# One stationary tile for both token halves: pair scores of a gated recurrence with the second half laid out in reverse

## The chip, the cores and the metric

The kernel runs on one core of a Trainium2 chip. The metric is the device time of one execution in microseconds (us), the median of several runs. The core has five engines with a queue each: TensorE (matmuls; PE in the profile, its weight loads PEld), VectorE (DVE), ScalarE (ACT), GpSimd (POOL), and SyncE (SP), which here issues the DMAs.

## What is computed

One layer of a streaming encoder on 1024 tokens of width 1024, all in float32: half a SwiGLU feed-forward block, a mixer with two groups of heads side by side, cross attention to 256 memory tokens, and another half block. The change is in the mixer. Its first group is a gated linear recurrence (4 heads of width 128), its second stick-breaking attention (8 heads of width 64). Cut to what matters:

```python
# recurrent heads: f is a gate per token and channel, k = 1 - f
#   S_t = diag(f_t) S_{t-1} + outer(k_t, i_t),    o_t = S_t^T q_t
# within a chunk this is
a = jnp.einsum('bhtd,bhsd,bhtsd->bhts', qt, kt, decay)      # decay = product of the gates between s and t, s <= t
o_intra = jnp.einsum('bhts,bhsv->bhtv', a, vt)
o_inter = jnp.einsum('bhtd,bhdv->bhtv', qt * jnp.exp(bt), state)
new_state = jnp.exp(b_last)[..., None] * state + jnp.einsum('bhsd,bhsv->bhdv', k_dec, vt)

# stick-breaking heads, strictly causal, z = q.k / sqrt(d)
#   A[t,s] = sigmoid(z_ts) * prod_{s<j<t} (1 - sigmoid(z_tj)),    o = A v
```

## The kernel before, in words

Activations lie transposed: channels on the 128 partitions, tokens along the free dimension, in two halves of H = 512 tokens, so every tensor comes as a half 0 and a half 1 (`hf`). Projections are sums of three matmuls (`mm3`, lines 125 to 129) of operands split into a high and a low part; a matmul on plain float32 operands appears in the profile as two instructions.

The mixer runs over four pairs p of stick-breaking heads and four recurrent heads n, woven by `interleave` (lines 142 to 150): it runs one generator step by step and between its steps a due share of a second generator's units. For each p there are two stages (lines 1443 to 1457). In the attention stage `sb_attend(p)` is woven with the projection `hg_proj(p)` of recurrent head p (48 units). In the recurrent stage `hg_attend(p)` (30 steps) is woven with `sb_proj(p + 1)` (64 units of three or six matmuls); for the last head with `memory()`, the projection of the memory tokens (128 units). The order on each engine's queue is settled when the kernel is built, from source order and dependencies.

**`hg_attend`** (lines 1281 to 1377) treats chunks of 128 tokens (index j, four to a half). Scores between a query and a key need the product of the gates between them, and the kernel builds these by doubling. `scores` (line 1289) gives the plain products, of which the diagonal is kept (line 1319) in a tile A per half, keys on partitions, queries along the free dimension. Then, for m = 1, 2, 4, ..., 64, neighbouring blocks of m tokens form pairs: a key of the first block of a pair meets a query of the second. `pair_scores(hf, m)` computes these scores. For m up to 16 (line 1309) it multiplies all 128 keys of a chunk, as the stationary operand, with the 64 queries that lie in second blocks (picked with strides), and VectorE copies the valid blocks into A with a predicated copy and a mask (line 1313). For m of 32 and 64 (line 1302) it multiplies only the m keys of one block with the m queries of its partner, block by block, and ScalarE copies each result to A (line 1304). After each level VectorE multiplies the queries of the second blocks by the product of the gates of their partner (line 1330), the keys of the first blocks likewise (line 1331), and the products of the gates pairwise (line 1333). All this is done for half 0 and then for half 1 at each level, one step of the weave each. At the end the keys are transposed (line 1340), and the state is carried from chunk to chunk in order of time (lines 1345 to 1363).

Each level's matmuls use as stationary operand keys of one half, of which at m up to 16 only every other block is a key block; the masks drop the rest.

**`sb_attend`** (lines 1103 to 1239): for each block t of 128 queries `z_steps` computes the scores with all earlier keys, two sigmoids, masks the diagonal block on GpSimd (line 1129), forms the running product from the latest key to the earliest with a scan over a reversed view (line 1132) and multiplies (line 1134). A query block of half 1 does this first for the keys of half 1, then for those of half 0, with the product carried over. `turn` transposes the weights, `values` multiplies them with v.

The masks of `pair_scores` are made at the start on GpSimd (lines 513 to 522): 5 fills and 10 selects of 128x64.

Of the kernel before, what the change touches and what calls it, by code (L numbers as in the profile page):

```python
# [18 lines left out]
P = 128  # L19
T = 1024  # L20
# [11 lines left out]
def hybrid_layer(ctx, tc, x, x_cols, mem, gains, ffn1_w_gu, ffn1_w_down, w_in, w_out, mem_w_q, mem_w_kv, mem_w_o,  # L32
# [397 lines left out]
    with ExitStack() as st:  # L430
# [83 lines left out]
        for m in (1, 2, 4, 8, 16):  # L514
            mk = maskp.tile([P, P // 2], F32, name=f"mask{m}")
            nc.gpsimd.memset(mk, 1.0)
            nb = P // (2 * m)
            nc.gpsimd.affine_select(out=mk, in_=mk, compare_op=ALU.is_ge, fill=0.0, base=0,
                                    pattern=[[-2 * m, nb], [0, m]], channel_multiplier=1)
            nc.gpsimd.affine_select(out=mk, in_=mk, compare_op=ALU.is_ge, fill=0.0, base=m - 1,  # L520
                                    pattern=[[2 * m, nb], [0, m]], channel_multiplier=-1)
            masks[m] = mk
# [518 lines left out]

    def sb_proj(p, r):
# [24 lines left out]
        for jj in range(4):  # L1067
            ps = psa.tile([P, 2, 2 * P], F32, name="acc")
            for q in range(2):
                t0 = (2 * jj + q) % 4 * P  # L1070
                hh = hT[jj // 2]
                for k in range(DC):
                    wh, wl = units[k // 4]
                    lhs = (hh[k][0][:, t0:t0 + P], hh[k][1][:, t0:t0 + P])
                    mm3(ps[:, q, :], lhs, (wh[:, k % 4, :], wl[:, k % 4, :]), k == 0, k == DC - 1)
                    if k % 2:
                        yield
            v = sbk.tile([P, 2, 2 * P], F32R, name=("v0h", "v0l", "v1h", "v1l")[jj])
            iv = hgp.tile([P, 2, P], F32, name=f"i{jj}")
            for q in range(2):  # L1080
                y = ys[jj // 2][:, (2 * jj + q) % 4:(2 * jj + q) % 4 + 1]
# [21 lines left out]
    def sb_attend(p, r, rest):  # L1103
# [5 lines left out]
        def z_steps(hf, e, g):  # L1109
            for t in (2 * g, 2 * g + 1):  # L1110
                width = (t + 1) * P
                carry = None
                qs = slice(t % 4 * P, t % 4 * P + P)
                q = r["q", t // 4][e]
                for s0 in ((0,) if width <= H else (H, 0)):
                    n = min(width - s0, H)
                    nn = max(n, 2 * P)
                    k, kl = r["k", s0 // H][e], r["kl", s0 // H][e]
                    z = psz.tile([P, H], F32, name="z")
                    nc.tensor.matmul(z[:, 0:nn], q[:, qs], k[:, 0:nn], start=True, stop=False)  # L1120
                    nc.tensor.matmul(z[:, 0:nn], q[:, qs], kl[:, 0:nn], start=False, stop=True)
                    om = sbp.tile([P, H], F32, name="om", bufs=2)
                    b = b_tile(p)
                    nc.scalar.activation(om[:, 0:n], z[:, 0:n], AF.Sigmoid, scale=-0.125)  # L1124
                    nc.scalar.activation(b[:, 0:n], z[:, 0:n], AF.Sigmoid, scale=0.125)
                    if carry is None:
                        dg = slice(n - P, n)
                        for a, fill in ((om, 1.0), (b, 0.0)):
                            nc.gpsimd.affine_select(out=a[:, dg], in_=a[:, dg], compare_op=ALU.is_gt, fill=fill,  # L1129
                                                    base=0, pattern=[[-1, P]], channel_multiplier=1)  # L1130
                    rev = om[:, n - 1::-1]
                    nc.vector.tensor_tensor_scan(rev, rev, rev, 1.0 if carry is None else carry,  # L1132
                                                 op0=ALU.mult, op1=ALU.bypass)
                    nc.vector.tensor_tensor(b[:, 0:n - 1], b[:, 0:n - 1], om[:, 1:n], op=ALU.mult)
                    if carry is not None:
                        nc.vector.tensor_tensor(b[:, n - 1:n], b[:, n - 1:n], carry, op=ALU.mult)
                    carry = om[:, 0:1]
# [3 lines left out]
        def turn(hf, e, g, jj):  # L1141
# [3 lines left out]
            offs = {2 * jj: 2 * P if diag else 0, 2 * jj + 1: 0 if diag else 2 * P}  # L1145
            for j in (2 * jj, 2 * jj + 1):
                for t in (2 * g, 2 * g + 1):
                    if j > t:
                        continue
                    c0 = offs[j] + (t % 2) * P  # L1150
                    nc.tensor.transpose(tr[:, c0:c0 + P], w[hf, e, t, j // 4][:, j % 4 * P:j % 4 * P + P], ident)
            lo = P if diag else 0
            wh = sbk.tile([P, H], F32R, name="wh", bufs=2)
            wl = sbk.tile([P, H], F32R, name="wl", bufs=2)
            if diag:
                nc.gpsimd.memset(wh[:, 0:P].bitcast(F32), 0.0)
                nc.gpsimd.memset(wl[:, 0:P].bitcast(F32), 0.0)
            nc.scalar.activation(wh[:, lo:H], tr[:, lo:H], AF.Copy)
            nc.vector.tensor_tensor(wl[:, lo:H], tr[:, lo:H], wh[:, lo:H].bitcast(F32), op=ALU.subtract)
            return wh, wl, offs  # L1160

        def values(hf, e, g, jj, turned, first):
            wh, wl, offs = turned
            for j in (2 * jj, 2 * jj + 1):
                ws = slice(offs[j], offs[j] + 2 * P)
                vv = r["v", jj][:, j % 2, e * P:(e + 1) * P]
                oo = halfway[hf, e][:, g % 2 * 2 * P:(g % 2 + 1) * 2 * P]
# [84 lines left out]
    def hg_proj(n, r):  # L1252
        uq, uf, ug = [load_cols(mw, w_in, [c0 + P * n]) for c0 in (0, 512, 1536)]
        for hf in range(2):
            ps = psa.tile([P, H], F32, name="acc")
            yield from proj_steps(ps, uq, hT[hf])
            r["hq", hf] = hgp.tile([P, H], F32, name="hq", bufs=2)
            nc.vector.tensor_tensor(r["hq", hf], ps, rs[hf], op=ALU.mult)
        for hf in range(2):
            ps = psa.tile([P, H], F32, name="acc")  # L1260
            yield from proj_steps(ps, uf, hT[hf])
            f = hgp.tile([P, H], F32, name="hf", bufs=2)
            k = hgp.tile([P, H], F32, name="hk", bufs=2)
# [4 lines left out]
            r["hf", hf], r["hk", hf] = f, k  # L1268
        for hf in range(2):
# [3 lines left out]
            sg = hgp.tile([P, H], F32, name="hA", bufs=2)  # L1273
# [7 lines left out]
    def hg_attend(n, r):  # L1281
        sl = [slice(j * P, (j + 1) * P) for j in range(4)]
        A, tots = {}, {}

        def scores(hf):
            a = psz.tile([P, H], F32, name="z")
            k, q = r["hk", hf], r["hq", hf]
            for j in range(4):
                nc.tensor.matmul(a[:, sl[j]], k[:, sl[j]], q[:, sl[j]], start=True, stop=True)
            return a.rearrange("p (j t) -> p j t", j=4)  # L1290

        def pair_scores(hf, m):
# [3 lines left out]
            k = r["hk", hf]  # L1296
            if m >= 32:
                for b in range(nb):
                    rows = slice(2 * m * b, 2 * m * b + m)
                    for j in range(4):  # L1300
                        k0 = j * P + 2 * m * b
                        nc.tensor.matmul(a[rows, j * m:(j + 1) * m], k[:, k0:k0 + m], r["hq", hf][:, k0 + m:k0 + 2 * m],
                                         start=True, stop=True)
                    nc.scalar.activation(A[hf][rows, :, 2 * m * b + m:2 * m * (b + 1)],
                                         a[rows, 0:4 * m].rearrange("p (j t) -> p j t", j=4), AF.Copy)
                return
            q = r["hq", hf].rearrange("p (j b h r) -> p j b h r", j=4, h=2, r=m)[:, :, :, 1, :]
            for j in range(4):
                nc.tensor.matmul(a[:, j * 64:(j + 1) * 64], k[:, sl[j]], q[:, j], start=True, stop=True)  # L1309
            dst = A[hf].rearrange("p j (b h r) -> p j b h r", h=2, r=m)[:, :, :, 1, :]  # L1310
            src = a[:, 0:4 * 64].rearrange("p (j b r) -> p j b r", j=4, r=m)
            mk = masks[m].bitcast(U32).unsqueeze(1).broadcast_to([P, 4, 64]).rearrange("p j (b r) -> p j b r", r=m)
            nc.vector.copy_predicated(dst, mk, src)

        for hf in range(2):
            A[hf] = hgp.tile([P, 4, P], F32, name="hA", bufs=2)
            a = scores(hf)
            q, f = r["hq", hf], r["hf", hf]
            nc.vector.tensor_tensor(A[hf], a, ident.unsqueeze(1).broadcast_to([P, 4, P]), op=ALU.mult)
            nc.vector.tensor_tensor(q, q, f, op=ALU.mult)  # L1320
            tots[hf] = f
            yield
        for m in (1, 2, 4, 8, 16, 32, 64):
            for hf in range(2):
                nb = H // (2 * m)
                tv = tots[hf].rearrange("p (b h) -> p b h", h=2)
                qv = r["hq", hf].rearrange("p (b h r) -> p b h r", h=2, r=m)[:, :, 1, :]
                kv = r["hk", hf].rearrange("p (b h r) -> p b h r", h=2, r=m)[:, :, 0, :]
                pair_scores(hf, m)
                nc.vector.tensor_tensor(qv, qv, tv[:, :, 0:1].broadcast_to([P, nb, m]), op=ALU.mult)  # L1330
                nc.vector.tensor_tensor(kv, kv, tv[:, :, 1:2].broadcast_to([P, nb, m]), op=ALU.mult)
                nt = r["hf", hf][:, 0:nb]
                nc.vector.tensor_tensor(nt, tv[:, :, 0], tv[:, :, 1], op=ALU.mult)
                tots[hf] = nt
                yield
        for hf in range(2):
            k = r["hk", hf]
# [7 lines left out]
        for hf in range(2):  # L1345
            o = pso.tile([P, H], F32, name="so")
            ds = psz.tile([P, H], F32, name="z")
            k, q = r["hk", hf], r["hq", hf]
            for j in range(4):
                iv = r["i", 2 * hf + j // 2][:, j % 2, :]  # L1350
                nc.tensor.matmul(ds[:, sl[j]], k[:, sl[j]], iv, start=True, stop=True)
                nc.tensor.matmul(o[:, sl[j]], iv, A[hf][:, j, :], start=True, stop=state is None)
# [5 lines left out]
                else:  # L1358
                    nc.vector.scalar_tensor_tensor(ns, state, tots[hf][:, j:j + 1], ds[:, sl[j]], op0=ALU.mult, op1=ALU.add)
# [347 lines left out]
```

## Time and profile before

| | |
|---|---|
| median of 3 runs | 2291.49 us (2290.48 to 2295.58) |
| the profiled execution | 2291.69 us; span from first to last instruction 2290.0 us, mean granted TensorE clock 0.992 |
| TensorE matmul busy | 2216.7 us, 97% of the span |
| VectorE, ScalarE, GpSimd busy | 73%, 43%, 32% |
| recurrent heads 0 to 3 | about 791 to 856, 934 to 995, 1073 to 1134, 1212 to 1290 us |
| attention pairs 1 to 3 | about 856 to 934, 995 to 1073, 1134 to 1212 us |

How to read it: a row of a group or a timeline names engine, source line, operation, output tile <- input tiles, shapes, and a count (x8: eight instructions in a row). In a timeline the first number is the start in us from the span's start, the second the time until the last of the group ends; for TensorE ends are modelled, so distances between starts are what counts. "[0.93 <-PE z L1309]" is idle time of the engine ahead of the instruction and what ended it. L82 and L127 to L129 are lines of helpers. The stage borders above are read off the timeline, at the first scores of a head and the first work of the next pair.

### The profile page before, as it was taken

Reading aid. Unit: us, or ns where it says so; the run is one execution under the profiler, and the core shown is the slowest. Engines: PE = TensorE matmul, PEld = TensorE weight load, DVE = VectorE, ACT = ScalarE, POOL = GpSimd, SP = SyncE. Lnnn points to the kernel's source line nnn. Section 1 sums busy time; section 2 is a strip of 40 time slices with the busy share of each in tenths; the row PEclk is TensorE's granted clock in tenths of the full one; section 3 lists DMA queues with packets and bytes.
Section 4 is the critical chain, followed back from the end, with each engine's and each line's share of the span. In section 5 each row is a group of like instructions: output and inputs, shape, how many; then the busy total and the mean of one; then the engine's idle time right before and its main releaser. Section 6 shows DMA issues by size and latency. Waiting matters only on the chain.

```text
span 2290.0 us, 31245 instructions
## 1 busy us (share of the span) xinstructions
PE 2216.7 (97%) x11240; PEld 1858.3 (81%) x11240; DVE 1677.4 (73%) x2816; ACT 984.7 (43%) x1877; POOL 728.6 (32%) x685
## 2 busy tenths in 40 slices
PE   8999999999999999999989999999999999999997
PEld 6788888878778797888979888888778888887876
DVE  6877777867976869778697536666687676786896
ACT  6444434443345536344464334223454343444324
POOL 3463535335541102010032020001356353533553
PEclk9999999999989999999999999999999999999999
DMA  8343434766721001100115311110333333376552
GB/s 294 111 143 126 151 126 146 253 223 202 242 92 38 28 20 28 32 25 28 38 29 164 113 37 56 47 37 33 134 111 115 116 133 118 131 254 232 190 175 74
DMA packets 220571, 265.80 MB, mean 116 GB/s; under 512 B 13440, under 2 KB 144512, under 8 KB 220416
## 3 DMA queue, kind: packets, MB, share of 16 engines
q1 hardware_dynamic: 220416, 263.80, 34.8%
q8 instruction: 89, 1.46, 0.3%
q14 instruction: 66, 0.54, 0.1%
HBM read 187.47 MB, written 76.28 MB: 115 GB/s over the span
## 4 chain that ended last, share of the span: by engine, by line
PE 79%; DVE 11%; ACT 3%; issue 3%; DMA 3%; POOL 1%; SPq 0%; POOLq 0%; DVEq 0%; ACTq 0%
PE X L82 25%; PE Y L82 13%; PE Z L82 6%; PE acc L127 5%; PE acc L129 5%; PE acc L128 5%; DVE E L82 2%; PE q L128 2%; PE q L127 2%; PE q L129 2%; PE z L1309 1%; DVE f L82 1%; DVE om L1132 1%; PE wo L129 1%; PE wo L127 1%
## 5 line engine op out<-in xcount | busy, mean ns | idle before, releaser
L82 PE MATMUL X<-T,f 128*128 128x512 f32 x1464 | 343.7, 390 | 0.3 <-DVE T L82 0.2
L82 PEld LDWEIGHTS X<-T,f 128*128 128x128 f32 x1464 | 274.3, 188 | 58.7 <-DVE T L82 1.2
L82 PE MATMUL X<-hh,f 128*128 128x512 f32 x975 | 313.6, 392 | 5.6 <-ACT E L82 3.5
L82 ACT ACTIVATE f<-S 128x512 fp32r<-128x512 f32 (+2 forms) x256 | 155.3, 608 | 274.5 <-POOL S L82 261.1
L82 DVE TENSOR_TENSOR f<-S,f 128x512 fp32r<-128x512 f32 (+2 forms) x256 | 228.5, 905 | 31.1 <-ACT f L82 29.7
L82 PEld LDWEIGHTS X<-hh,f 128*128 128x128 f32 x975 | 183.7, 188 | 46.7 <-ACT E L82 4.4
L82 POOL TENSOR_TENSOR E<-E,rs 128x512 f32<-128x512 f32 x100 | 164.6, 1646 | 124.6 <-DVE E L82 110.2
L82 DVE TENSOR_TENSOR f<-r,f 128x512 fp32r<-128x512 f32 (+2 forms) x192 | 203.5, 1077 | 0.1
L82 PE MATMUL X<-hl,f 128*128 128x512 f32 x488 | 191.4, 392 | 3.6 <-DVE hl L82 3.6
L82 POOL TENSOR_TENSOR S<-r,r 128x512 f32<-128x512 f32 (+2 forms) x64 | 91.1, 1423 | 307.7 <-DMA r<-in_ffn_w_gu_dram 93.6
L82 PE MATMUL Y<-T,f 128*128 128x512 f32 x732 | 176.4, 389 | 0.0
L82 PE MATMUL Y<-hh,f 128*128 128x512 f32 x488 | 160.9, 389 | 0.1
L82 PEld LDWEIGHTS Y<-T,f 128*128 128x128 f32 x732 | 137.4, 188 | 28.7
L82 PE MATMUL Z<-hh,f 128*128 128x512 f32 x488 | 160.6, 389 | 0.0
L127 PE MATMUL acc<-hh,wh 128*128 128x512 f32 (+1 forms) x384 | 153.4, 400 | 3.5 <-DVE E L82 3.5
L128 PE MATMUL acc<-hl,wh 128*128 128x512 f32 (+1 forms) x384 | 145.3, 378 | 2.2 <-DMA hl<-msl 2.2
L129 PE MATMUL acc<-hh,wl 128*128 128x512 f32 (+1 forms) x384 | 145.4, 379 | 0.0
L82 POOL TENSOR_TENSOR S<-S,r 128x512 f32<-128x512 f32 (+2 forms) x64 | 83.2, 1299 | 185.0 <-DVE f L82 151.6
L1129 POOL TENSOR_SCALAR_AFFINE_SELECT om<-om 128x128 f32<-128x128 f32 x64 | 27.1, 423 | 356.7 <-ACT om L1124 356.4
L82 DVE TENSOR_TENSOR E<-X,E 128x512 f32<-128x512 f32 x98 | 67.3, 687 | 95.6 <-PE X L82 95.0
L82 ACT ACTIVATE E<-X 128x512 f32<-128x512 f32 x102 | 60.5, 593 | 165.7 <-PE X L82 165.6
L107 ACT ACTIVATE wh<-wraw 128x512 fp32r<-128x512 f32 (+1 forms) x128 | 79.0, 654 | 106.9 <-PE acc L128 39.7
(454 smaller groups left out, 5492.1 us busy)
## 6 DMA issues: line engine op xcount, KB each, us to landing
r<-in_ffn_w_gu_dram SPq DMA_DIRECT2D x86, 512.0 KB, 3.6
r<-in_ffn_w_down_dram SPq DMA_DIRECT2D x32, 512.0 KB, 4.2
wraw<-in_w_in_dram SPq DMA_DIRECT2D x20, 512.0 KB, 3.7
wraw<-in_mem_w_kv_dram SPq DMA_DIRECT2D x16, 512.0 KB, 3.8
x<-in_x_cols_dram SPq DMA_DIRECT2D x16, 256.0 KB, 5.4
T<-in_x_dram SPq DMA_DIRECT2D x8, 512.0 KB, 6.3
fx<-x SPq DMA_DIRECT2D x16, 256.0 KB, 5.1
sg<-fx SPq DMA_DIRECT2D x16, 256.0 KB, 4.1
```

The source lines that it names most:

```text
L82: done = getattr(self.eng, name)(*args, **kw)
L107: nc.scalar.activation(hi[:, part], src[:, part], AF.Copy)
L127: nc.tensor.matmul(ps, lh, rh, start=start, stop=False)
L128: nc.tensor.matmul(ps, lh, rl, start=False, stop=False)
L129: last_mm[0] = nc.tensor.matmul(ps, ll, rh, start=False, stop=stop).ins
L1129: nc.gpsimd.affine_select(out=a[:, dg], in_=a[:, dg], compare_op=ALU.is_gt, fill=fill, base=0, pattern=[[-1, P]], channel_multiplier=1)
L1132: nc.vector.tensor_tensor_scan(rev, rev, rev, 1.0 if carry is None else carry, op0=ALU.mult, op1=ALU.bypass)
L1309: nc.tensor.matmul(a[:, j * 64:(j + 1) * 64], k[:, sl[j]], q[:, j], start=True, stop=True)
```

## The change

The host lays the second half of the tokens out in reverse: position 512 + i holds token 1023 - i; the outputs are turned back on the host, outside the measured time. In half 1 the second block of a pair, in time, is now the first in memory. So at each level the key blocks of half 0 are the even ones and those of half 1 the odd ones, and together they fill one 128x128 tile. `pair_scores(m)` copies them into such a tile `keys` (one ScalarE copy of 128x512, all four chunks), multiplies it by the 64 + 64 queries of both halves, four matmuls per level at all seven levels, and copies the valid quarter for each half into A as before: two predicated copies for m up to 16, ScalarE copies of blocks for 32 and 64. The queries, keys, gates and A of the two halves lie in one tile each, and each update of line 1330, 1331 or 1333 becomes one instruction over both halves. A level still has two steps in the weave: pair scores and query update in the first, key and gate update in the second. The masks are 128 x (number of pairs), one set per half, and are broadcast over m.

The stick-breaking heads follow the new order: for keys of half 1 the scan runs forwards, the diagonal block stands first, and the positions of blocks are turned (`place`). The diff, cut:

```diff
+        for hf in range(2):
+            for m in (1, 2, 4, 8, 16):
+                nb = P // (2 * m)
+                mk = maskp.tile([P, nb], F32, name=f"mask{hf}_{m}")
+                nc.gpsimd.memset(mk, 1.0)
+                for sign, base in ((1, -m * hf), (-1, m * hf + m - 1)):
+                    nc.gpsimd.affine_select(out=mk, in_=mk, compare_op=ALU.is_ge, fill=0.0, base=base,
+                                            pattern=[[-2 * m * sign, nb]], channel_multiplier=sign)
+                masks[hf, m] = mk.bitcast(U32).unsqueeze(1).unsqueeze(3).broadcast_to([P, 4, nb, m])
...
+    def place(t):
+        return t if t < 4 else 7 - t
...
                 for s0 in ((0,) if width <= H else (H, 0)):
+                    back = s0 == H
...
-                    rev = om[:, n - 1::-1]
-                    nc.vector.tensor_tensor_scan(rev, rev, rev, 1.0 if carry is None else carry,
+                    run = om[:, 0:n] if back else om[:, n - 1::-1]
+                    nc.vector.tensor_tensor_scan(run, run, run, 1.0 if carry is None else carry,
                                                  op0=ALU.mult, op1=ALU.bypass)
...
     def hg_proj(n, r):
+        for name in ("hq", "hf", "hk", "hA"):
+            r[name] = hgp.tile([P, 2, H], F32, name=name)
...
-        def pair_scores(hf, m):
+        def pair_scores(m):
             a = psz.tile([P, H], F32, name="z")
             nb = P // (2 * m)
-            if m >= 32:
...
-                        nc.tensor.matmul(a[rows, j * m:(j + 1) * m], k[:, k0:k0 + m], r["hq", hf][:, k0 + m:k0 + 2 * m],
-                                         start=True, stop=True)
...
-                nc.tensor.matmul(a[:, j * 64:(j + 1) * 64], k[:, sl[j]], q[:, j], start=True, stop=True)
-            nc.vector.copy_predicated(dst, mk, src)
+            keys = sbp.tile([P, H], F32, name="om", bufs=2)
+            nc.scalar.activation(keys.rearrange("p (b h r) -> p b h r", h=2, r=m), view(K, 0, (2 * m, 4 * nb), (H + m, 2), (1, m)),
+                                 AF.Copy)
+            for j in range(4):
+                queries = view(Q, j * P + m, (H - m, 2), (2 * m, nb), (1, m))
+                nc.tensor.matmul(a[:, sl[j]], keys[:, sl[j]], queries, start=True, stop=True)
+            a = a.rearrange("p (j e b r) -> p j e b r", j=4, e=2, r=m)
+            for hf in range(2):
+                dst = A[:, hf].rearrange("p (j b h r) -> p j b h r", j=4, h=2, r=m)[:, :, :, 1 - hf, :]
+                if m < 32:
+                    nc.vector.copy_predicated(dst, masks[hf, m], a[:, :, hf])
+                    continue
                 for b in range(nb):
+                    rows = slice(2 * m * b + m * hf, 2 * m * b + m * hf + m)
+                    nc.scalar.activation(dst[rows, :, b], a[rows, :, hf, b], AF.Copy)
...
         for m in (1, 2, 4, 8, 16, 32, 64):
+            nb = H // (2 * m)
+            pair_scores(m)
+            qv, kv = view(Q, m, (H - m, 2), (2 * m, nb), (1, m)), view(K, 0, (H + m, 2), (2 * m, nb), (1, m))
+            nc.vector.tensor_tensor(qv, qv, view(F, 0, (H + 1, 2), (2, nb), (0, m)), op=ALU.mult)
+            yield
+            nc.vector.tensor_tensor(kv, kv, view(F, 1, (H - 1, 2), (2, nb), (0, m)), op=ALU.mult)
+            pairs = F[:, :, 0:2 * nb].rearrange("p e (b h) -> p e b h", h=2)
+            nc.vector.tensor_tensor(F[:, :, 0:nb], pairs[:, :, :, 0], pairs[:, :, :, 1], op=ALU.mult)
+            yield
...
+    x = np.concatenate([x[:H], x[H:][::-1]])
```

More of the change, by code (lines that the diff above doesn't have):

```diff
@@ L513, in hybrid_layer @@
         masks = {}
[L514 to L522, printed above, removed]
+        for hf in range(2):
[7 more added lines that the diff above has]
+                masks[hf, m] = mk.bitcast(U32).unsqueeze(1).unsqueeze(3).broadcast_to([P, 4, nb, m])
     def lower_bound(after):
@@ L1069, in sb_proj @@
             for q in range(2):
-                t0 = (2 * jj + q) % 4 * P
+                t0 = place(2 * jj + q) * P
                 hh = hT[jj // 2]
@@ L1080, in sb_proj @@
             for q in range(2):
-                y = ys[jj // 2][:, (2 * jj + q) % 4:(2 * jj + q) % 4 + 1]
+                t0 = place(2 * jj + q)
+                y = ys[jj // 2][:, t0:t0 + 1]
                 vh = v[:, q, :].rearrange("p (a b) -> p a b", b=64)[:, 0::3, :]
@@ L1112, in z_steps @@
                 carry = None
-                qs = slice(t % 4 * P, t % 4 * P + P)
+                qs = slice(place(t) * P, place(t) * P + P)
                 q = r["q", t // 4][e]
                 for s0 in ((0,) if width <= H else (H, 0)):
+                    back = s0 == H
                     n = min(width - s0, H)
                     nn = max(n, 2 * P)
+                    ks = slice(H - nn, H) if back else slice(0, nn)
                     k, kl = r["k", s0 // H][e], r["kl", s0 // H][e]
@@ L1119, in z_steps @@
                     z = psz.tile([P, H], F32, name="z")
-                    nc.tensor.matmul(z[:, 0:nn], q[:, qs], k[:, 0:nn], start=True, stop=False)
-                    nc.tensor.matmul(z[:, 0:nn], q[:, qs], kl[:, 0:nn], start=False, stop=True)
+                    nc.tensor.matmul(z[:, 0:nn], q[:, qs], k[:, ks], start=True, stop=False)
+                    nc.tensor.matmul(z[:, 0:nn], q[:, qs], kl[:, ks], start=False, stop=True)
+                    z = z[:, nn - n:nn] if back else z[:, 0:n]
@@ L1144, in turn @@
             tr = pst.tile([P, H], F32, name="tr")
-            offs = {2 * jj: 2 * P if diag else 0, 2 * jj + 1: 0 if diag else 2 * P}
+            swapped = diag and hf == 0
+            offs = {2 * jj: 2 * P if swapped else 0, 2 * jj + 1: 0 if swapped else 2 * P}
             for j in (2 * jj, 2 * jj + 1):
@@ L1149, in turn @@
                         continue
-                    c0 = offs[j] + (t % 2) * P
-                    nc.tensor.transpose(tr[:, c0:c0 + P], w[hf, e, t, j // 4][:, j % 4 * P:j % 4 * P + P], ident)
-            lo = P if diag else 0
+                    c0 = offs[j] + place(t) % 2 * P
+                    s0 = (j if j < 4 else t - j) * P
+                    nc.tensor.transpose(tr[:, c0:c0 + P], w[hf, e, t, j // 4][:, s0:s0 + P], ident)
             wh = sbk.tile([P, H], F32R, name="wh", bufs=2)
             wl = sbk.tile([P, H], F32R, name="wl", bufs=2)
+            full, blank = slice(0, H), None
             if diag:
[L1156 to L1159, printed above, removed]
+                full, blank = (slice(0, H - P), slice(H - P, H)) if hf else (slice(P, H), slice(0, P))
+                nc.gpsimd.memset(wh[:, blank].bitcast(F32), 0.0)
+                nc.gpsimd.memset(wl[:, blank].bitcast(F32), 0.0)
+            nc.scalar.activation(wh[:, full], tr[:, full], AF.Copy)
+            nc.vector.tensor_tensor(wl[:, full], tr[:, full], wh[:, full].bitcast(F32), op=ALU.subtract)
             return wh, wl, offs
@@ L1261, in hg_proj @@
             yield from proj_steps(ps, uf, hT[hf])
[L1262 to L1263 removed]
+            f, k = r["hf"][:, hf], r["hk"][:, hf]
             nc.vector.tensor_tensor(f, ps, rs[hf], op=ALU.mult)
@@ L1272, in hg_proj @@
             gs = hgp.tile([P, H], F32, name="hg", bufs=2)
-            sg = hgp.tile([P, H], F32, name="hA", bufs=2)
+            sg = r["hA"][:, hf]
             nc.vector.tensor_tensor(gs, ps, rs[hf], op=ALU.mult)
@@ L1282, in hg_attend, with view @@
         sl = [slice(j * P, (j + 1) * P) for j in range(4)]
-        A, tots = {}, {}
+        A, Q, K, F = r["hA"], r["hq"], r["hk"], r["hf"]
+        def view(t, at, *dims):
+            return bass.AP(t.tensor, t.offset + at, [list(t.ap[0]), *map(list, dims)])
         def scores(hf):
             a = psz.tile([P, H], F32, name="z")
-            k, q = r["hk", hf], r["hq", hf]
             for j in range(4):
-                nc.tensor.matmul(a[:, sl[j]], k[:, sl[j]], q[:, sl[j]], start=True, stop=True)
-            return a.rearrange("p (j t) -> p j t", j=4)
@@ L1292, in pair_scores @@
-        def pair_scores(hf, m):
+                nc.tensor.matmul(a[:, sl[j]], K[:, hf, sl[j]], Q[:, hf, sl[j]], start=True, stop=True)
+            return a
+        def pair_scores(m):
             a = psz.tile([P, H], F32, name="z")
             nb = P // (2 * m)
-            k = r["hk", hf]
-            if m >= 32:
-                for b in range(nb):
[L1299 to L1302, printed above, removed]
-                                         start=True, stop=True)
[L1304 to L1313, printed above, removed]
@@ L1347, in hg_attend @@
             ds = psz.tile([P, H], F32, name="z")
-            k, q = r["hk", hf], r["hq", hf]
-            for j in range(4):
-                iv = r["i", 2 * hf + j // 2][:, j % 2, :]
+            k, q = K[:, hf], Q[:, hf]
+            for i in range(4):
+                j = place(4 * hf + i)
+                iv = r["i", 2 * hf + i // 2][:, i % 2, :]
                 nc.tensor.matmul(ds[:, sl[j]], k[:, sl[j]], iv, start=True, stop=True)
-                nc.tensor.matmul(o[:, sl[j]], iv, A[hf][:, j, :], start=True, stop=state is None)
+                nc.tensor.matmul(o[:, sl[j]], iv, A[:, hf, sl[j]], start=True, stop=state is None)
                 if state is not None:
```

51 lines of the change are left out of this document (20 added, 31 removed).

## The prediction

> **What bounds the kernel now.** I read the page first, then busy time by stage, then TensorE's timeline inside one stage of the recurrent heads, because the change is mostly there.
>
> ```profile
> PE 2216.7 (97%) x11240; PEld 1858.3 (81%) x11240; DVE 1677.4 (73%) x2816; ACT 984.7 (43%) x1877; POOL 728.6 (32%) x685
> ```
>
> TensorE has work for 97% of the span of 2290.0 us. That is a mean over many stages, so the next view cuts out the second head pair: a stage of stick-breaking attention (856 to 934 us), the stage of recurrent head 1 with the next pair's projection (934 to 995), and the last recurrent head with the memory projection (1212 to 1290). After the colon come PE, PEld, DVE, ACT and POOL busy us.
>
> ```profile
> 856.00:934.00 78.00, 73.46 (x427) 61.30 (x426) 67.83 (x138) 45.32 (x98) 16.80 (x47) 1.00 0.10 28
> 934.00:995.00 61.00, 61.00 (x456) 55.49 (x455) 41.92 (x121) 18.22 (x39) 0.21 (x1) 1.00 0.09 27
> 1212.00:1290.00 78.00, 72.66 (x615) 69.94 (x614) 60.42 (x160) 30.80 (x60) 4.24 (x3) 1.00 0.50 152
> ```
>
> In the recurrent stage PE is busy for all 61.00 us, VectorE for 41.92 and ScalarE for 18.22, and the view of PE's waits is empty there (also for heads 0 and 2). So this stage is as long as TensorE's queue, and a matmul taken out of it shortens it, as long as nothing new makes PE wait. In the last head's stage PE is idle for 5.3 of 78 us, which I leave as they are. In the attention stage VectorE (67.83 of 78) is close to the bound instead.
>
> **The matmuls.** Modelled ends say nothing of cost, so I take start-to-start distances: from the last projection matmul ahead of a group to the second one behind it, less two ordinary distances. First the scores, 128 queries against 128 keys; each float32 matmul is two instructions, so four of them are x8.
>
> ```profile
> 791.77 0.40 PE L129 MATMUL acc<-hh,wl 128*128 128x512 f32 x1
> 792.00 1.05 PE L1289 MATMUL z<-hq,hk 128*128 128x128 f32 x8
> 792.81 0.48 PE L127 MATMUL acc<-hh,wh 128*128 128x512 f32 x1
> 793.13 0.40 PE L128 MATMUL acc<-hl,wh 128*128 128x512 f32 x1
> ```
>
> Then the pair scores of one token half at m=1, four matmuls with only 64 queries each:
>
> ```profile
> 799.73 0.39 PE L129 MATMUL acc<-hh,wl 128*128 128x512 f32 x1
> 799.97 1.00 PE L1309 MATMUL z<-hq,hk 128*128 128x64 f32 x8
> 800.77 0.48 PE L127 MATMUL acc<-hh,wh 128*128 128x512 f32 x1
> 801.09 0.39 PE L128 MATMUL acc<-hl,wh 128*128 128x512 f32 x1
> ```
>
> Both are 1.36 us from first to last row. Two ordinary distances are 0.46 (791.77 to 792.00 is 0.23), so each group costs 0.90 us: 64 columns cost as much as 128. This is the core of the forecast: the changed kernel asks 128 queries of each stationary tile, for both halves at once, and pays 0.90 once where it paid it twice. Next, m=32 (four matmuls with 32 keys as stationary) and m=64:
>
> ```profile
> 821.22 0.40 PE L129 MATMUL acc<-hh,wl 128*128 128x512 f32 x1
> 821.55 0.44 PE L1302 MATMUL z<-hq,hk 128*32 128x32 f32 x8
> 821.92 0.50 PE L127 MATMUL acc<-hh,wh 128*128 128x512 f32 x1
> 822.25 0.40 PE L128 MATMUL acc<-hl,wh 128*128 128x512 f32 x1
> 822.58 0.44 PE L1302 MATMUL z<-hq,hk 128*32 128x32 f32 x8
> 822.95 0.50 PE L129 MATMUL acc<-hh,wl 128*128 128x512 f32 x1
> ```
>
> ```profile
> 829.83 0.28 PE L129 MATMUL acc<-wh,hl 128*128 128x256 f32 x1
> 830.04 0.68 PE L1302 MATMUL z<-hq,hk 128*64 128x64 f32 x8
> 830.65 0.39 PE L127 MATMUL acc<-wh,hh 128*128 128x256 f32 x1
> 830.87 0.28 PE L128 MATMUL acc<-wl,hh 128*128 128x256 f32 x1
> 830.99 0.28 PE L129 MATMUL acc<-wh,hl 128*128 128x256 f32 x1
> ```
>
> At m=32 a group costs 1.03 less 0.46, 0.57 us; at m=64 it costs 1.04 (829.83 to 830.87) less two distances of 0.12, as the last two rows stand apart: 0.80.
>
> Removed per head: five levels of two halves, 10 x 0.90 = 9.0; m=32, two halves of two blocks, 4 x 0.57 = 2.3; m=64, 2 x 0.80 = 1.6; together 12.9. Added: seven levels, 7 x 0.90 = 6.3. Net 6.6 us per head, 26.3 for four (unrounded).
>
> A rule of the Trainium skill speaks against folding m=32 into the full array: TensorEngine Tiling (Array Packing), Overview, gives up to a fourfold speedup to a stationary side of at most 32 columns. By it the four small groups together would cost about 0.9 us (an estimate), and the net would fall from 26.3 to about 20.8; the trace's 0.57 a group does not show that speedup, so the sum keeps 2.3 (by the rule the result would be 2273).
>
> **The chain that the change builds.** Before, the halves take turns, so one half's updates run while PE works for the other. Now a level is one chain over both: ScalarE copies the keys, PE multiplies, VectorE does two predicated copies, the query update, the key update, and the next level's copy waits for that. Its parts:
>
> ```profile
> 801.00 0.73 DVE L1313 COPY_PREDICATED hA<-mask,z 128x256 f32<-128x256 uint32 x1 [0.93 <-PE z L1309]
> 801.54 0.20 DVE L163 SCALAR_TENSOR_TENSOR u<-u,ms 128x8 f32<-128x8 f32 x1
> ```
>
> ```profile
> 808.37 0.44 DVE L1313 COPY_PREDICATED hA<-mask,z 128x256 f32<-128x256 uint32 x1
> 808.70 0.29 DVE L1333 TENSOR_TENSOR hf<-hf 128x128 f32<-128x128 f32 x1
> ```
>
> ```profile
> L1320 DVE TENSOR_TENSOR hq<-hq,hf x8: 673/684/1756, 794.7 to 1216.6; 128x512 f32<-128x512 f32 x8
> ```
>
> ```profile
> L1052 ACT ACTIVATE sq<-acc 64x512 fp32r<-64x512 f32 x4 | 2.4, 593 | 9.8 <-DVE acc L1048 6.9 <-DVE sq L1054 2.9
> L107 ACT ACTIVATE wh<-wraw 128x512 fp32r<-128x512 f32 x4 | 2.3, 624 | 6.7 <-PE acc L128 6.7
> ```
>
> From the group's start (799.97) to the first predicated copy (801.00) is 1.03; a copy takes 0.54 at m=1 and 2, 0.33 from m=4 on; an update of 512 elements 0.68; the key copy is nearest to the ScalarE copy of 128x512 at 0.62. At m=1 and 2 that is 1.03+1.08+1.36+0.62 = 4.1 us; at 4 to 16, 3.7; at 32 and 64, where ScalarE does the copying out, 3.0. What covers it: a level has two steps with 64/30 projection units each, three matmuls of 0.23 per unit, 2.9 us, and its own 0.90: 3.8 (in the last head 128/30 units of three matmuls of 0.12 a step, 3.1, so 4.0). So the cover is short by 0.3 at m=1 and 2, 0.26 x 2 x 4 = 2.1 us, unless PE takes a later unit meanwhile; the row at 822.58, where a pair group stands between two matmuls of one unit, shows that the order isn't tied to the source. Bounds 0 and 2.1; I charge 2.1, because hand-overs aren't counted. A gain is excluded, since there is no PE wait to remove.
>
> **The rest, at nothing.** VectorE's updates halve in number and double in width, in a stage where it has 19 us to spare. ScalarE gets 28 more copies of 0.62, 4.3 us a head beside 18.22 of 61; queued behind a waiting copy are the weight splits and the projection's copies. The queries, keys, gates and scores of both halves now share tiles, so the next head's first write waits for both halves; it comes 8 of 48 units into a 78 us stage, 13 us in. The attention edits keep every count and size and only turn directions; I take nothing for that, and a bound for scans stands below.
>
> ```profile
> L518 POOL TENSOR_SCALAR_AFFINE_SELECT mask<-mask x5: 354/647/654, 3.7 to 7.7; 128x64 f32<-128x64 f32 x5
> 13.90 1.73 POOL L79 TENSOR_TENSOR S<-x,x 128x512 f32<-128x512 f32 x1 [5.12 <-DMA x<-in_x_cols_dram]
> ```
>
> Masks: 20 selects on GpSimd in place of 10, of 64 down to 4 columns. At 0.65 each they would run 6.5 us longer and eat the 5.12 us of slack ahead of the first sum, 1.4 us late at worst; narrower tiles make it nothing.
>
> **Sum.** 26.3 less 2.1 is 24.2. The profiled execution took 2291.69, so 2267.5; the median of three is 0.2 below it: 2267.
>
> **The rivals.** *The chain sets the pace.* VectorE and ScalarE also serve the projection, in order. In 796 to 832 us:
>
> ```profile
> L1048 DVE TENSOR_TENSOR acc<-acc,rs 128x512 f32<-128x512 f32 x4 | 2.8, 694 | 0.0
> L1054 DVE TENSOR_TENSOR sq<-acc,sq 64x512 fp32r<-64x512 f32 x4 | 2.8, 688 | 0.1
> L1063 DVE TENSOR_TENSOR skl<-acc,sk 64x512 fp32r<-64x512 f32 x4 | 2.8, 688 | 1.3 <-ACT sk L1056 1.3
> L108 DVE TENSOR_TENSOR wl<-wraw,wh 128x512 fp32r<-128x512 f32 x4 | 2.7, 684 | 0.0
> ```
>
> These 11.1 us in 36, scaled to seven levels of 3.8 us, are 1.2 us a level. If all of it falls into the chain and PE finds nothing else, a level is short by 1.4, 1.0 and 0.4 us (two, three and two levels): 6.7 a head, 27 in all, and the saving is gone: 2292. With the 4.7 us on ScalarE above, scaled alike, 0.5 a level, 14 more: 2306. It decides from 0.94 us of wait per level on. For it: the handing over four times. Against: the key update needs only the key copy, not PE, so it can go ahead of the predicated copies; and the stage now has VectorE idle a third of the time. Chance 0.16 (0.09 slower, 0.06 within the bound, 0.01 faster).
>
> *The wider moving side costs.* The 128-query row is of contiguous queries; the new ones come in runs of m. At 64 columns a slow read would be hidden in the 0.90. If strided reads ran at half speed, 0.8 us more at each of five levels, 16 us: 2283. Chance 0.10. The Trainium skill, Advanced Engine Details and Errata, SBUF Cachelines, asks for two hits on a 16-byte line: the queries at m=1, eight bytes apart, have them, but the key copy at m=1, which changes halves with every element, does not. By that the queries would read at full speed, the copy might take double at m=1, four times 0.62, and the result be 2270 (an estimate). No run here shows either.
>
> *Scanning forwards is cheaper.*
>
> ```profile
> L1132 DVE TENSOR_TENSOR_SCAN om<-om x96: 405/1084/1312, 703.2 to 1194.6; 128x512 f32<-128x512 f32 x48, 128x128 f32<-128x128 f32 x16, 128x256 f32<-128x256 f32 x16, 128x384 f32<-128x384 f32 x16
> ```
>
> All scans run backwards now, at (1312-405)/384 = 2.4 ns an element. A third of the scans turn forwards, 2 x 1280 elements a head pair; at half the price 12 us less on VectorE, near the bound in those stages: 2255. Nothing shows a forward scan, and one that is dearer is no more excluded, so I take 0 in the sum; chance 0.06. That the change doesn't do what it says I leave out: the matmul count follows from the code.
>
> **The numbers.** Forecast 0.68, own range 2263 to 2273: below, the 2.1 us of short cover not paid (2265) and 0.1% of spread; above, the masks' 1.4, a doubled key copy at m=1, 2.5, and the spread. A measurement of this kernel tells about 0.2%, 4.6 us, from no change. Faster by more than that: 0.68+0.10+0.06+0.01, 0.85; within: 0.06; slower: 0.09. The range runs from the third rival's 2255 to 2288, past the second one's 2283 and just beyond the edge of what can be told from no change (2287); the chain rival is left out.
>
> **What would show it.** 224 pair-score instructions on TensorE, each group of eight still 0.90 us; recurrent stages near 55 us instead of 61; PE waiting for the key copy under 0.3 us a level; scans unchanged; attention stages still 78 us. It is wrong if PE's waits on the key copy or the query update reach a microsecond per level, or if groups at m=1 and 2 stand wider than at m=16.

## The result and the profile after

| | before | after |
|---|---|---|
| median | 2293.09 us (2290.48 to 2295.58, 4 runs) | 2271.64 us (2267.67 to 2275.52, 4 runs) |
| profiled execution | 2291.69, span 2290.0 | 2270.07, span 2268.3 |

The ratio is 0.9906 with an interval of 0.9884 to 0.9929: 21.5 us faster, where 24.2 were forecast.

The page of the kernel after, first part:

```profile
PE 2196.8 (97%) x10952; PEld 1840.6 (81%) x10952; DVE 1665.5 (73%) x2732; ACT 1003.3 (44%) x1905; POOL 732.3 (32%) x700
```

TensorE has 288 instructions fewer and is still busy for 97%. To see where the time went I cut both spans at the first scores of each recurrent head (a head's period: its stage and the next attention stage). Busy time by stretch of the kernel before, then of the kernel after; the number ahead of the comma is the length in us:

```profile
792.00:930.40 138.40, 133.86 (x875) 116.19 (x874) 109.63 (x256) 63.17 (x137) 17.00 (x48) 1.00 0.10 28
930.40:1068.74 138.34, 133.81 (x875) 116.19 (x874) 109.61 (x256) 63.22 (x137) 17.01 (x48) 1.00 0.09 28
1068.74:1210.56 141.82, 134.19 (x876) 116.14 (x875) 113.02 (x256) 68.23 (x146) 28.37 (x54) 1.00 0.15 44
1210.56:2290.00 1079.44, 1048.04 (x5098) 874.97 (x5096) 744.66 (x1206) 421.25 (x780) 340.36 (x242) 0.99 0.36 119
```

```profile
790.07:924.07 134.00, 128.27 (x803) 111.01 (x802) 108.11 (x235) 67.93 (x144) 17.08 (x48) 1.00 0.10 28
924.07:1058.07 134.00, 128.25 (x803) 111.00 (x802) 108.11 (x235) 67.94 (x144) 17.08 (x48) 1.00 0.10 28
1058.07:1194.46 136.39, 130.02 (x804) 112.32 (x802) 110.45 (x235) 73.19 (x153) 28.91 (x54) 0.99 0.15 46
1194.46:2268.30 1073.84, 1043.41 (x5026) 871.67 (x5024) 742.73 (x1185) 424.51 (x786) 341.16 (x242) 0.99 0.36 119
```

The periods shrink by 4.4, 4.3 and 5.4 us, the stretch from the last head's scores to the end by 5.6; the other 1.9 of 21.7 lie ahead of the first scores, whose start varies from 789.0 to 793.2 us in the profiles of this case. The first two periods repeat to 0.1 us in every profile of one kernel, so they are the ruler for the experiments. The other two stretches are a coarser measure: the third period of the kernel before holds a wait of 2.5 us that this profile of the change lacks, and TensorE's granted clock over the first 80 us of the last head was 1.00 before and 0.96 here (see the last section). The third set's profile of the change, below, has that wait and a clock of 1.00; there the two shrink by 3.0 and 8.5 us, 11.5 together instead of 11.0. Inside a period the saving lies in the recurrent stage: from the first scores to the last matmul on A it is 59.6 us before and 55.2 after, and the rest is 78.8 in both.

The instructions of two lines of the kernel after, the pair scores and the scans (least/median/most ns, first and last start):

```profile
L1316 PE MATMUL z<-hq,om x224: 270/275/415, 794.9 to 1230.8; 128*128 128x128 f32 x112
...
L1139 DVE TENSOR_TENSOR_SCAN om<-om x96: 406/1085/1311, 701.3 to 1179.5; 128x512 f32<-128x512 f32 x48, 128x128 f32<-128x128 f32 x16, 128x256 f32<-128x256 f32 x16, 128x384 f32<-128x384 f32 x16
```

224 pair-score instructions, and scans as long as before, forwards or backwards. What is new is in TensorE's waits in the recurrent stage of head 1 (930 to 985 us; us in total, times, longest), where the view was empty before:

```profile
PE z L1316 <- ACT om L1312: 0.8, 1, 0.8
PE tr L1032 <- DVE yy L1028: 0.5, 1, 0.5
```

Both stand in the same place in heads 0, 1 and 2. TensorE's timeline shows the first one in head 0, at m=64:

```profile
819.52 0.39 PE L129 MATMUL acc<-hh,wl 128*128 128x512 f32 x1
820.67 1.16 PE L1316 MATMUL z<-hq,om 128*128 128x128 f32 x8 [0.76 <-ACT om L1312]
821.58 0.48 PE L127 MATMUL acc<-hh,wh 128*128 128x512 f32 x1
821.90 0.39 PE L128 MATMUL acc<-hl,wh 128*128 128x512 f32 x1
```

First to last row is 2.38; less two distances of 0.23 the group costs 1.92 instead of 0.90. The timelines of VectorE (one row: the update that the copy needs) and ScalarE say why:

```profile
816.86 0.69 DVE L1339 TENSOR_TENSOR hk<-hk,hf 128x512 f32<-128x512 f32 x1
```

```profile
816.42 0.59 ACT L1055 ACTIVATE sk<-acc 64x512 fp32r<-64x512 f32 x1
817.02 0.59 ACT L1059 ACTIVATE sk<-acc 64x512 fp32r<-64x512 f32 x1
817.62 0.59 ACT L1055 ACTIVATE sk<-acc 64x512 fp32r<-64x512 f32 x1
818.23 0.59 ACT L1059 ACTIVATE sk<-acc 64x512 fp32r<-64x512 f32 x1
818.85 1.11 ACT L1325 ACTIVATE hA<-z 32x128 f32<-32x128 f32 x4
819.98 0.63 ACT L1312 ACTIVATE om<-hk 128x512 f32<-128x512 f32 x1
```

The keys are updated by 817.55 (816.86 + 0.69), but the copy (L1312) starts at 819.98: in ScalarE's queue it stands behind four copies of the next pair's projection and the four block copies of m=32.

The same distances for all seven levels of head 1 are, from m=1 on, 1.59, 0.91, 0.89, 0.90, 1.04, 1.04 and 1.92 (the first holds eight small matmuls of the projection, L1021; in the kernel before it reads 1.48), together 8.3 where the kernel before has 13.4. The m=16 group starts 0.14 us after VectorE's query update ends, and those of m=32 and 64 start 0.05 after the key copy ends. In the last head the groups from m=16 on cost 0.89 to 0.90.

### The profile page after: what moved, and what is told of

It is laid out like the page before. It is cut to its first block, busy times and chain, and to the rows that moved or that the text cites. A ratio compares the mean times of both kernels' runs of the same rounds, so it can differ in the third digit from the quotient of the medians.

```text
span 2268.3 us, 30628 instructions
## 1 busy us (share of the span) xinstructions
PE 2196.8 (97%) x10952; PEld 1840.6 (81%) x10952; DVE 1665.5 (73%) x2732; ACT 1003.3 (44%) x1905; POOL 732.3 (32%) x700
## 4 chain that ended last, share of the span: by engine, by line
PE 77%; DVE 12%; ACT 3%; DMA 3%; issue 2%; POOL 1%; SPq 0%; POOLq 0%; DVEq 0%; ACTq 0%
PE X L82 26%; PE Y L82 13%; PE Z L82 6%; PE acc L127 4%; PE acc L129 4%; PE acc L128 4%; PE q L128 2%; PE q L127 2%; PE q L129 2%; DVE om L1139 2%; DVE f L82 1%; DVE E L82 1%; PE wo L129 1%; PE wo L127 1%; PE wo L128 1%
```

## The experiments

All times are medians in us; the periods are those of heads 0, 1 and 2 in the profiled run.

**The change again.** The changed kernel unaltered, once in the first set of runs and once in the third.

> The changed kernel again, as the control for the runs beside it: 2271.6 us in the first measurement, 21.5 below the kernel before. Expected 0.988 to 0.993 of the kernel before.

2269.61, ratio 0.9909 [0.9895, 0.9923]; periods 134.0, 134.0, 136.3. The third set:

> The changed kernel once more, as the measure for the two runs beside it: 2270 (2268 to 2275), head periods 134.0, 134.0 and 136.4 us as in the first two profiles of it.

2271.35, ratio 0.9909 [0.9896, 0.9921]; periods 134.0, 134.0 and 138.8, which the last section takes up.

**The new order alone.** Second half reversed, attention turned, but pair scores and updates half by half as before:

```diff
 def pair_scores(hf, m):
...
+    q = r["hq", hf].rearrange("p (j b h r) -> p j b h r", j=4, h=2, r=m)[:, :, :, 1 - hf, :]
     for j in range(4):
         nc.tensor.matmul(a[:, j * 64:(j + 1) * 64], k[:, sl[j]], q[:, j], start=True, stop=True)
```

> Half 1 reversed and the attention heads in the new order, but the recurrent heads as before: a tile per half, updates per half, pair scores per half. Theory (the saving is the matmul groups of the pair scores, the layout is neutral): as slow as the kernel before, 2293 within 5 us. Rival (the saving comes from the new order itself, such as scans that run forwards): 2272 to 2280.

2295.01, ratio 1.0016 [1.0006, 1.0026]. Its second period, by stretch:

```profile
929.84:1068.93 139.09, 134.38 (x875) 116.42 (x874) 109.75 (x256) 63.23 (x137) 17.07 (x48) 1.00 0.09 27
```

VectorE is busy for 109.75 us, before 109.61. Turning a third of the scans forwards saves nothing, and the order alone costs some 0.7 us a period, all of it in the recurrent stage (60.3 us instead of 59.6); what costs it was not found. The rival of cheaper forward scans falls.

**Shared tiles and merged updates, separate pair scores.**

```diff
 def pair_scores(m):
-    keys = sbp.tile([P, H], F32, name="om", bufs=2)
...
+    for hf in range(2):
+        a = psz.tile([P, H], F32, name="z")
...
+        for j in range(4):
+            nc.tensor.matmul(a[:, j * 64:(j + 1) * 64], K[:, hf, sl[j]], q[:, j], start=True, stop=True)
```

> The whole change, except that the pair scores are multiplied per half again, with the keys of one half as the stationary side and small blocks at 32 and 64; no key copy. Queries, keys and gates of both halves stay in one tile, with one update over both. Theory: TensorE sets the pace, so fewer VectorE instructions bring nothing: 2293 within 5 us, and the pair groups are back at 0.90, 0.57 and 0.80. Rival (the merged updates give the saving): 2272 to 2280.

2289.18, ratio 0.9990 [0.9982, 0.9999]; the second period:

```profile
927.73:1065.66 137.93, 133.29 (x875) 115.80 (x874) 108.41 (x235) 63.16 (x137) 17.07 (x48) 1.00 0.10 28
```

21 VectorE instructions fewer than the run above and 1.2 us less of period; the intervals of the two runs don't overlap (the medians are 5.8 us apart), so this is small but real. It is not shown to come from the merged updates, because the order of the small groups changed as well. Both halves now stand in one step, and at m=32 and 64 some groups stand in a row:

```profile
957.75 0.59 PE L1324 MATMUL z<-hq,hk 128*32 128x32 f32 x16
965.16 0.97 PE L1324 MATMUL z<-hq,hk 128*64 128x64 f32 x16
```

The two levels cost 2.9 us here (0.71 + 0.56 + 0.56 + 1.09) and 3.8 in the run above, which is 0.9 of the 1.2. Against the kernel before the period is only 0.4 us shorter. The shared stationary tile itself brings the other 3.9, from 137.93 to 134.00.

**128 queries in the kernel before.** Each group at m up to 16 is made as wide as the new ones, the number of groups unchanged:

```diff
-            q = r["hq", hf].rearrange("p (j b h r) -> p j b h r", j=4, h=2, r=m)[:, :, :, 1, :]
+            q = r["hq", hf].rearrange("p (j b h r) -> p j h b r", j=4, h=2, r=m)
             for j in range(4):
-                nc.tensor.matmul(a[:, j * 64:(j + 1) * 64], k[:, sl[j]], q[:, j], start=True, stop=True)
+                nc.tensor.matmul(a[:, sl[j]], k[:, sl[j]], q[:, j], start=True, stop=True)
```

> The kernel before, where the pair scores up to m=16 multiply all 128 queries of a chunk instead of the 64 of the second blocks, read in the same strided runs of m; 40 groups of eight instructions in all, nothing else changed. Theory (a group is paced by its stationary loads, 64 columns cost as much as 128): no change, within 2 us of the kernel before, groups still 0.90. Rival (the moving side costs, strided above all): up to 0.8 us a group, 8 to 32 us slower.

2294.34, ratio 1.0003 [0.9995, 1.0012]. A group in TensorE's timeline of that kernel (half 1 at m=1):

```profile
800.31 0.39 PE L129 MATMUL acc<-hh,wl 128*128 128x512 f32 x1
800.54 1.07 PE L1309 MATMUL z<-hq,hk 128*128 128x128 f32 x8
801.36 0.48 PE L127 MATMUL acc<-hh,wh 128*128 128x512 f32 x1
801.68 0.40 PE L128 MATMUL acc<-hl,wh 128*128 128x512 f32 x1
```

1.37 less 0.46 is 0.91, with 128 strided queries; with 64 it was 0.90. Its first two periods are 138.65 and 138.67, 0.3 above those of the kernel before: forty groups twice as wide cost next to nothing, some 0.03 us each.

**Contiguous queries in the changed kernel.** The moving side reads half 0's queries as they lie.

```diff
-                queries = view(Q, j * P + m, (H - m, 2), (2 * m, nb), (1, m))
+                queries = Q[:, 0, sl[j]]
```

> The changed kernel with the moving side of the pair scores replaced by 128 contiguous queries of half 0, so the scores are other numbers; same count and size. Theory: the groups at m=1 cost what they cost at m=16, so the groups keep about 0.90 and m=1 loses at most 0.1. Rival (strided reads are paid): groups at m=1 and 2 become 0.1 us or more shorter, and the time falls with them.

One run: 2271.59, periods 133.9, 133.9, 136.3. TensorE at m=1 of this kernel, then of the changed one:

```profile
795.48 0.39 PE L129 MATMUL acc<-hh,wl 128*128 128x512 f32 x1
795.71 1.05 PE L1316 MATMUL z<-hq,om 128*128 128x128 f32 x8
...
797.41 0.49 PE L127 MATMUL acc<-hh,wh 128*128 128x512 f32 x1
```

```profile
794.61 0.39 PE L129 MATMUL acc<-hh,wl 128*128 128x512 f32 x1
794.87 1.14 PE L1316 MATMUL z<-hq,om 128*128 128x128 f32 x8
...
796.66 0.48 PE L127 MATMUL acc<-hh,wh 128*128 128x512 f32 x1
```

1.93 against 2.05 from first to last row: 0.12 us at m=1, and 0.02 or less at m=2 and 4. Little of that is the stride. In the changed kernel the first matmul of the m=1 group starts 0.26 after the row ahead instead of 0.23, and the second one 0.19 after the first instead of 0.11, as at m=16, 32 and 64, where the group also waits. The other distances between its matmuls differ by 0.002 from those with contiguous queries, about 0.01 in all. VectorE's timeline of the changed kernel shows what the group waits for:

```profile
794.04 0.68 DVE L1331 TENSOR_TENSOR hq<-hq,hf 128x512 f32<-128x512 f32 x1
```

This is the query update of half 1, which ends 0.15 us before the group starts, as in heads 1 and 2. With half 0's queries alone the group doesn't need it, so this run took away a wait along with the strides. That the wait is for this update is read off the timeline. In the kernel before, the same strides cost 0.01. The rival of the wider moving side, 0.8 us a group, falls.

**The key copy made twice.** The same copy is issued again at each level.

```diff
+            for _ in range(2):
                 nc.scalar.activation(keys.rearrange(...), view(K, 0, ...), AF.Copy)
```

> The changed kernel with every key copy made twice into the same tile, 28 more ScalarE copies of 0.63 us. Theory (the copy is late at the levels 16, 32 and 64 of heads 0 to 2 and hidden elsewhere): 9 x 0.63, 4 to 7 us slower than the changed kernel. Rival A (hidden everywhere): no change. Rival B (on the path at every level): 28 x 0.63, 17 us slower.

2277.05, ratio 0.9926 [0.9912, 0.9939]; its second period:

```profile
926.11:1060.26 134.15, 128.19 (x803) 111.04 (x802) 108.16 (x235) 72.54 (x151) 17.16 (x48) 1.00 0.10 28
```

4.6 us more on ScalarE move the period by 0.15; the wait at m=64 of head 1 grows from 0.77 to 0.97. So the copy's own length is nearly hidden; what TensorE waits for is the copy's place in the queue. The median is 5 to 7 us above the change's, but the intervals overlap, the first two periods don't show it, and the unaltered change was not run in this set. That this copy costs more elsewhere is not shown.

**Keys early.** The key update goes ahead of the predicated copies, and the next level's copy right behind it, before the block copies of its own level:

```diff
+            def ahead():
+                nc.vector.tensor_tensor(kv, kv, view(F, 1, (H - 1, 2), (2, nb), (0, m)), op=ALU.mult)
+                if m < 64:
+                    keys.append(copy_keys(2 * m))
+            pair_scores(m, keys.pop(), ahead)      # calls ahead() behind its four matmuls
```

> The changed kernel with the key update and the next level's key copy placed right behind a level's matmuls, ahead of the predicated copies and the query update; same instructions. Theory (the missing part of the forecast is PE waiting for key copies at the levels 16 to 64, about 1.3 us a head): those waits go, 3 to 5 us faster than the changed kernel, 2267 to 2269. Rival (the wait only moves to the query update or to ScalarE's queue): within 2 us of the changed kernel.

2272.6, ratio 0.9915 [0.9902, 0.9928]: 3 us above the change in the same set, where 3 to 5 below was expected. Again, beside the change on one chip:

> The early key copies once more, beside the changed kernel on the same chip. Theory (the key copy's wait costs about 1.2 us in each head, and the rest of the kernel doesn't give it back): four heads by 1.1 are 4.4 us, so 2266 where the change takes 2270; in the profile the first two head periods 132.8 and 133.0 again, and the last one, 137.7 in the first look, back at 136. Rival (the last head gives it back, because there the memory projection's VectorE work stands behind the early key update): again 137.7 in the last period, and the total within 2 us of the change.

2272.0, ratio 0.9910 [0.9895, 0.9924]; its first three periods, and m=64 of head 0 in TensorE's timeline:

```profile
791.63:924.39 132.76, 127.78 (x803) 111.16 (x802) 107.99 (x235) 67.78 (x144) 17.08 (x48) 1.00 0.10 29
924.39:1057.46 133.07, 128.12 (x803) 111.13 (x802) 108.00 (x235) 67.80 (x144) 17.08 (x48) 1.00 0.10 29
1057.46:1195.11 137.65, 129.54 (x804) 112.43 (x803) 111.40 (x235) 72.93 (x153) 28.48 (x54) 0.99 0.16 45
```

```profile
820.91 0.39 PE L129 MATMUL acc<-hh,wl 128*128 128x512 f32 x1
821.14 1.05 PE L1320 MATMUL z<-hq,om 128*128 128x128 f32 x8
821.94 0.48 PE L127 MATMUL acc<-hh,wh 128*128 128x512 f32 x1
822.26 0.40 PE L128 MATMUL acc<-hl,wh 128*128 128x512 f32 x1
```

1.35 less 0.46 is 0.89: the wait is gone, at m=32 too, and the periods are shorter by 1.2 and 0.9, in both runs. That shows the place in the queue as the cause of the wait at these two levels. At m=16 the group still costs 1.02 to 1.08: there it waits for the query update, which this order leaves behind the predicated copies. The total doesn't follow: 0.7 us above the control of the same set, where 4 below was expected. To see whether the last head gives the gain back:

```diff
+            if n < 3:
                 pair_scores(m, keys.pop(), ahead)
+            else:
+                pair_scores(m, copy_keys(m), lambda: None)
```

> The keys are updated and copied early in heads 0 to 2; the last head keeps the order of the change. Rival (the last head gives the gain back): head periods 132.8, 133.0, about 135.3 and three heads' gain in the total, 3.3 us below the change, about 2267. Theory (the last period's 137.7 was a chance of that run): the last period is 1.1 better than 136.4 at its start and the total lies 1.1 us above the kernel with early copies in all four heads.

2271.07, ratio 0.9906 [0.9894, 0.9919]; periods 132.8, 133.1, 137.7. The third period stayed at 137.7; it ends before the last head's pair scores, and the control of the same set has 138.8 there, so the last head's order isn't what holds it. The profiles with 137.7 and the one with 138.8 all have the 2.5 us wait of the last section, which the two profiles of the change with 136.4 and 136.3 lack: like for like, the early keys gain 1.1 in the third period too. Both versions tie with the change within some 3 us, and no version here beats it measurably. From the third head's scores to the end, the change takes 1210.2, 1210.9 and 1209.7 in its three profiles, the early keys 1210.0, 1213.0 and 1208.9 (the last one with the change's order in the last head): a gain of 2 us in the first two heads drowns in that. From the last head's scores to the end, at a clock of 1.00 over its first 80 us, the change takes 1071.0, early keys in three heads 1071.2 and in all four 1072.4; at 0.96 the change takes 1073.8 and 1074.5, early keys in all four 1075.3. That hints that some 1 us is given back in the last head, but these are single profiles: it stays open.

**Blocks at 32 and 64.** The shared tile only up to m=16; above, small blocks, those of one half in a row at m=32 and of both halves at m=64:

```diff
-            pair_scores(m)
+            (shared_scores if m < 32 else block_scores)(m)
```

> The changed kernel with small block matmuls per half at levels 32 and 64 and the shared tile only up to 16. Theory: these two levels cost 2.3+1.6 us a head as blocks and about 3.0 with the shared tile and its waits, so 2 to 5 us slower than the changed kernel. Rival (column tiles run side by side, or the waits there were all that the sharing brought): equal or faster.

2275.72, ratio 0.9921 [0.9908, 0.9934]; periods 133.9, 133.9, 136.3: as the change. TensorE, first half at m=32 and then m=64 in head 0:

```profile
817.71 0.39 PE L129 MATMUL acc<-hh,wl 128*128 128x512 f32 x1
818.02 0.59 PE L1333 MATMUL z<-hq,hk 128*32 128x32 f32 x16
818.55 0.50 PE L127 MATMUL acc<-hh,wh 128*128 128x512 f32 x1
818.88 0.39 PE L128 MATMUL acc<-hl,wh 128*128 128x512 f32 x1
...
825.26 0.28 PE L129 MATMUL acc<-wh,hl 128*128 128x256 f32 x1
825.47 0.97 PE L1333 MATMUL z<-hq,hk 128*64 128x64 f32 x16
826.36 0.38 PE L127 MATMUL acc<-wh,hh 128*128 128x256 f32 x1
826.59 0.28 PE L128 MATMUL acc<-wl,hh 128*128 128x256 f32 x1
```

Sixteen in a row cost 1.17 - 0.46 = 0.71 at m=32 (0.86 for the other half) and 1.33 - 0.24 = 1.09 at m=64, together 2.7; the change pays 1.04 + 1.92 there in head 1, with its wait. So sharing at these two levels brings nothing over blocks that stand in a row, as long as its copies are late; with the keys early it pays 0.89 + 0.89. The median is 4 to 6 us above the change's, with overlapping intervals and equal periods: not settled.

## Why the prediction was nearly right

- **The bound** held: 97% busy, and the time came out of the stage where matmuls were taken out; the attention parts kept 78.8 us.
- **0.90 for 64 or 128 columns** held: 0.91 in the kernel before with 128, and 0.89 to 0.91 at m=2 to 8 in the changed one. Without the small matmuls of the projection between them, the groups removed cost 12.7 us in head 1 instead of 12.9, because one group of m=32 and one of m=64 stand in a row in the kernel before and cost 1.25 together instead of 0.57 + 0.80.
- **The short cover** is the term of the sum that was mis-sized. The prediction charged 0.26 at m=1 and 2, "2.1 us" in all, from the length of the chain against the cover. In heads 0 to 2 TensorE loses, against 0.90 a group, 0.12 at m=1 and 0.14 at m=16 (by the timeline, behind VectorE's query update), 0.14 at m=32 and 1.02 at m=64 (behind the key copy), and 0.5 in a wait for VectorE's `yy`: 1.9 a head instead of 0.5. Hence 4.4 and 4.3 saved in heads 0 and 1, where 6.1 follow from the sum; with the 0.2 above, 0.1 to 0.2 is left without a cause. The step counted how long the chain is and overlooked the copy's place in ScalarE's queue: the prediction named what queues behind the copy, not what the copy queues behind. Keys early showed it for m=32 and 64. What delays `yy` was not tested.
- **The last head** differs: no wait at m=64. Heads 2 and 3 with all behind them save 11.0 us (11.5 like for like) where 12.1 were forecast.
- **The closeness of the total** is partly luck: by the profiles the heads save 19.8 of 24.2, and 1.9 more came from an earlier start.
- **The chain as a rival** did appear, but at one level: 0.76 us at m=64, above the 0.3 that the prediction had named as a sign, and 1.9 a head is 0.27 a level, far from the 0.94 from which it decides.
- **The rule of array packing** (the Trainium skill, TensorEngine Tiling (Array Packing), Overview) was set aside because the trace gave 0.57 for eight. In a row, eight more at 32 columns add 0.14 (0.71 - 0.57) or 0.29, against 0.90 on the full array: three to six times less, on both sides of its fourfold, though these groups also have fewer moving columns (32), so that packing alone isn't measured. A lone group of eight between matmuls of the full array hides it: half to three quarters of its 0.57 is there whether eight or sixteen stand in the row. The saving was still forecast from the right price, since the kernel before does pay 0.57.
- **The doubled copy at m=1** (the Trainium skill, Advanced Engine Details and Errata, SBUF Cachelines): the copy takes 0.86 at m=1, 0.71 at m=2 and 0.63 above, so a third more and not double. At m=1 it starts 15 us ahead of its matmuls and delays nothing.

## What to carry to other kernels

Where TensorE is the bound, count groups and what each costs by distances of starts; the second 64 moving columns were nearly free here. When a new helper copy goes onto another engine, read what stands ahead of it in that engine's queue at each place, not only how long it takes. Before folding small tiles into the full array, price them in a row: half or more of a lone small group's cost came with standing alone.

## What the runs showed of the hardware

Two things shift single runs by 2 to 3 us, as much as the smaller effects here. In the third attention stage VectorE instructions are held in some runs. VectorE in the third set's run of the changed kernel, then the same instruction in the first profile after:

```profile
1182.88 1.77 DVE L1144 TENSOR_TENSOR b<-b,om 128x511 f32<-128x511 f32 x1
1184.57 1.22 DVE L1146 TENSOR_TENSOR b<-b,om 128x1 f32<-128x1 f32 x1
```

```profile
1181.06 0.67 DVE L1144 TENSOR_TENSOR b<-b,om 128x511 f32<-128x511 f32 x1
```

One element takes 1.22 us (0.14 a few rows ahead), and 511 take 1.77 instead of 0.67, both beside three GpSimd products in a row (4.42 us from 1182.58 on); in the first profile after only the one-element instruction is held (1.26) and nothing waits long for it. There the 511 elements start 0.17 us before the three products (1181.06 and 1181.23), in the other run 0.30 after them. In the third set's run TensorE then waits 2.53 us for the result (L1183), and the period is 138.8 instead of 136.4. The kernel before and all three runs with early keys have the same wait of 2.5. That GpSimd causes it is read off the overlap and the order of starts, not tested.

And the granted TensorE clock over the first 80 us of the last head was 1.00 in the profile of the kernel before and in one of the change and 0.96 in the two others of the change, which take 1073.8 and 1074.5 us from there to the end where the one at 1.00 takes 1071.0.
